# A hybrid diffusion step on one core: the context's output projection and first FFN 2 weights beside the latents' attention, its second weights beside the latents' halves

## The chip, the cores and the metric

The kernel runs on one core of one Trainium2 chip. The metric is device time in microseconds of one execution. One execution was also recorded by the hardware profiler; all rows below come from it. TensorE is called PE in the rows (its weight loads PEld), VectorE DVE, ScalarE ACT, GpSimd POOL; SyncE (SP) issues all the transfers.

## What is computed

One layer of a hybrid backbone over 1024 latent tokens and 256 context tokens, model width 1024, all in fp32. A cut of the reference:

```
h = x + 0.5 * g1 * swiglu(modulate(rms_norm(x, ng[0]), sh1, sc1), ffn_w_in[0], ffn_w_out[0])
mix = mixer(modulate(rms_norm(h, ng[1]), sh2, sc2))     # four groups A, B, C, D of width 256, then @ w_out
h = h + g2 * mix
h = h + 0.5 * g3 * swiglu(modulate(rms_norm(h, ng[2]), sh3, sc3), ffn_w_in[1], ffn_w_out[1])
y = rms_norm(h, final_g)

def swiglu(x, w_in, w_out):
    a, b = jnp.split(x @ w_in, 2, axis=-1)
    return (jax.nn.silu(a) * b) @ w_out
```

Group A is windowed attention, B a long convolution (Hyena), C dense attention, D a gated linear recurrence (GLA). Context tokens see only context. Latents see latents, cached context keys (not those computed here) and given GLA states. So the context's and the latents' rows never need each other after the projections. The FFN's inner width is 2816, 22 blocks of 128.

## The kernel before

Activations lie with the model width on the partitions (8 blocks of 128) and tokens along the columns, in the three chunks of `CHUNKS`: latents 0 to 511, latents 512 to 1023, context (256 columns). A product in fp32 is made of three matmuls of rounded operands: a weight is split into a high part `wh` (ScalarE, line 56) and a low part `wl` (VectorE or GpSimd, line 62), the activation likewise, and `mm3` (lines 986 to 988) adds wh x xh, wh x xl and wl x xh in PSUM.

The kernel is written with a tile framework: pools hand out buffers, and a scheduler places each instruction on its engine's queue. It goes by priority: program order, and `tc.high_priority(offset=LEAD)` with LEAD = 4000 puts a block ahead by that many positions. Two blocks with the same offset keep their program order. Each engine then works its queue strictly in order. A pool with `side="right"` takes memory from the other end; memory and the eight PSUM banks are handed on only when their last reader is done.

The part of the program that the change touches, in program order:

1. Latents' attention and GLA (some 1500 to 1980 us). `run_gla` is written first, at plain priority; `run_attention(..., "lat")` after it at LEAD. Attention is four jobs, A and C with two pairs of heads each; in each, `attn_heads` loads keys and queries and makes each row's maximum (lines 690, 694), and `attn_core` makes scores, exponentials, sums (line 754) and values (line 742); the maxima of the next job run beside the core of the one before. GLA (`gla_prepare`, `gla`) first does the latents, then the context. PSUM: x=2, a=2, s=1, o=1 for attention, g=2 for GLA.
2. The context's output projection, `w_out(2, ...)`, on GLA's two banks, at plain priority. It reads the mixers' outputs (`ysc`), so it needs the context's GLA.
3. Then a new set of banks (l=6, h=1, a=1): the latents' output projection `w_out(0)`, `w_out(1)` with the sums of squares of its result (`sum_rsq`); beside it the context's norm (`norm_mod`).
4. `hidden_ctx`, the first weights of FFN 2 for the context: 22 steps of 48 matmuls of 256 columns, then SiLU (line 1021) and the product (line 1022). Four of its steps stand between the four steps of `halves`, which reads the latents' rows back, norms them (lines 1107, 1108) and splits the seven half-size operands (lines 1116, 62) that `hidden_lat` multiplies by a scheme of seven half-size products in place of eight.
5. `hidden_lat`, the first weights for the latents: 22 steps (some 2232 to 2640 us).
6. `second` for chunk 0, chunk 1 and the context: the second weights, 22 steps of 24 matmuls each, summed in eight banks (four for the context); the inner values come back from memory (`hid`). The final norm `finish(c)` of chunks 0 and 1 stands at steps 2 and 8 of the context's `second`, that of the context at the end. With `on_pe` (the last one) the squares are summed by matmuls (line 913), otherwise by VectorE and GpSimd with one matmul at the end (line 923); the bank comes from "h", which here is an alias of the eight "o" banks. Line 1679 and line 1677 make the output.

Of the kernel before, what the change touches and what calls it, by code (L numbers as in the profile page):

```python
# [9 lines left out]
F32 = mybir.dt.float32  # L10
# [827 lines left out]
def model(tc, i, o):  # L838
# [161 lines left out]
    def half_tiles(p):  # L1000
        return {n: tuple(p.tile([128, 4, 512], F32R, tag=n + r, name=n) for r in "hl") for n in HALVES}

    def hidden_ctx(P, idx, X, keep):

        W = {}

        def prepare(f):
            if f < NFF:
                with tc.high_priority(offset=LEAD if f else 0):
                    W[f] = [load_w(P, i["w1"][idx, f, s], lo_engines=("dve", "dve" if s else "pool"))  # L1010
                            for s in range(2)]
        prepare(0)
        yield
        for f in range(NFF):
            prepare(f + 1)
            ps = E.psum("l").rearrange("p (s t) -> p s t", s=2)
            for s, w in enumerate(W.pop(f)):
                mm3(ps[:, s], w, (at(X[0]), at(X[1])), 8)
            with tc.high_priority(offset=LEAD):
                g = P["t2"].tile([128, 512], F32, tag="t2", name="g")[:, :T_CTX]  # L1020
                nc.scalar.activation(out=g, in_=ps[:, 0], func=ACTF.Silu)
                nc.vector.tensor_tensor(out=g, in0=g, in1=ps[:, 1], op=ALU.mult)
                E.load(keep[f][:, T_LAT:], g)
            yield
# [116 lines left out]
            nc.tensor.matmul(ps, lhsT=E.ones128, rhs=t, start=k == 0, stop=k == 7)  # L1141
        rsqrt_into(E, None, R, ps, 1.0 / 1024, n, tiles=[work() for _ in range(3)], pin=True, sq_engine=nc.vector)

    def second(P, idx, c, keep, h):

        t0, n = CHUNKS[c]
        cd = cond_of(c)
        W = {}

        def prepare(f):  # L1150
            if f < NFF:
                with tc.high_priority(offset=LEAD):
                    g = P["gr"].tile([128, 512], F32, tag="gr", name="g")[:, :n]
                    E.load(g, keep[f][:, t0:t0 + n])
                    if n == 512:
                        gh, gl = (P["gs"].tile([128, 512], F32R, tag="gs", name="gs") for _ in range(2))
                    else:
                        both = P["gs"].tile([128, 512], F32R, tag="gs", name="gs")
                        gh, gl = both[:, :n], both[:, n:2 * n]
                    split_hi_lo(E, g, gh, gl, lo_engine="dve")  # L1160
                    W[f] = load_w(P, i["w2"][idx, f].rearrange("p (k m) -> p k m", k=8),
                                  lo_engines=("dve", "dve")), gh, gl
        per = 512 // n
        prepare(0)
        banks = [E.psum("o") for _ in range(8 // per)]
        for f in range(NFF):
            prepare(f + 1)
            (wh, wl), gh, gl = W.pop(f)
            for d in range(8):
                ps = banks[d // per][:, d % per * n:d % per * n + n]  # L1170
                first = f == 0 and d % per == 0
                mm3(ps, (lambda k: wh(d), lambda k: wl(d)), (lambda k: gh, lambda k: gl), 1, start=first,
                    stop=f == NFF - 1, loose=True)
            if f < NFF - 1:
                yield
        with tc.high_priority(offset=LEAD):
            for d in range(8):
                nc.vector.scalar_tensor_tensor(out=h[:, d], in0=banks[d // per][:, d % per * n:d % per * n + n],
                                               scalar=gates[:, idx, d, cd:cd + 1], in1=h[:, d], op0=ALU.mult, op1=ALU.add)
        yield  # L1180
# [394 lines left out]


    po = ExitStack()
    E.set_banks(po, x=2, a=2, s=1, o=1, g=2)
    ats = ExitStack()
    gls = ExitStack()  # L1580
    run_gla(E, gls)
    gls.close()
    cp = pool(ats, "atc", 1)
    E.ident_r, E.mask_r = cp.tile([128, 128], F32R, name="ident_r"), cp.tile([128, 640], F32R, name="mask_r")
# [7 lines left out]

    fs = ExitStack()
    P = dict(raw=pool(fs, "raw", 4, **R_), wb=pool(fs, "wb", 12, **R_), t2=pool(fs, "t2", 9, **R_))
    cs_ = ExitStack()
    xp2 = pool(cs_, "xn2", 1, **R_)
    Rl = [xp2.tile([128, 512], F32, name=f"rl{c}") for c in range(2)]
    hsc2 = scratch("hsc2", [1024, T_ALL])
    hv2 = hsc2.rearrange("(k p) t -> p k t", p=128)

# [21 lines left out]
            E.load(hv2[:, d, t0:t0 + n], t)  # L1622
            yield t

    h2st = ExitStack()
    h2 = pool(h2st, "h2", 1, **R_).tile([128, 8, T_CTX], F32, name="h2")
    Y = load_y(2, xp2)
    for _ in w_out(2, Y, "g", lambda d: h2[:, d]):
        pass
    ats.close()  # L1630
    po.close()
    po = ExitStack()
    E.set_banks(po, l=6, h=1, a=1)
    h = [None, None, h2]
    with ExitStack() as st:
        xp, hq = pool(st, "xy", 1), pool(st, "hq", 8)
        Y = [load_y(c, xp) for c in range(2)]
        Xc = norm_mod(P, xp2, h, 2, 2)
        for c in range(2):
            exp_ln_tables()  # L1640
            sum_rsq(P, w_out(c, Y[c], "l", lambda d: hq.tile([128, 512], F32, tag="hq", name="hq")), 512, Rl[c],
                    lambda: hq.tile([128, 512], F32, tag="hq", name="rs"))
    h2st.close()
    hst = ExitStack()
    XL = half_tiles(pool(hst, "xs", 1))
    xb = pool(cs_, "xb", 7, **R_)
    run = hidden_ctx(P, 1, Xc, hid[1])
    next(run)
    next(run)
    for _ in halves(P, 2, xb, lambda k, c: hv2[:, k, 512 * c:512 * c + 512], Rl, XL):  # L1650
        next(run)
    for _ in run:
        pass
    cs_.close()
    for _ in hidden_lat(P, 1, XL, hid[1]):
        pass
    po.close()
# [7 lines left out]
    def finish(c):  # L1665
        t0, n = CHUNKS[c]
        exp_ln_tables()
        last = c == len(CHUNKS) - 1
        with tc.high_priority(offset=LEAD if last else 0):
            R = chunk_rsq(P, h, c, xp.tile([128, 8 * n], F32, tag=f"tmp{c}", name="tmp"), on_pe=last)  # L1670
            out = xp.tile([128, 8, n], F32, tag=f"out{c}", name="out")
            for k in (1, 4, 7):
                nc.scalar.activation(out=out[:, k], in_=h[c][:, k], func=ACTF.Copy, scale=fing[:, k:k + 1])
            yv = o["y"].rearrange("(k p) t -> p k t", p=128)
            for k in range(8):
                if k % 3 == 1:
                    nc.gpsimd.tensor_tensor(out=out[:, k], in0=out[:, k], in1=R, op=ALU.mult)
                else:
                    nc.vector.scalar_tensor_tensor(out=out[:, k], in0=h[c][:, k], scalar=fing[:, k:k + 1], in1=R,
                                                   op0=ALU.mult, op1=ALU.mult)  # L1680
                if k % 2:
                    E.load(yv[:, k - 1:k + 1, t0:t0 + n], out[:, k - 1:k + 1])

    for c, (t0, n) in enumerate(CHUNKS):
        h[c] = hp.tile([128, 8, n], F32, name=f"h{c}")
        E.load(h[c], hv2[:, :, t0:t0 + n])
        for f, _ in enumerate(second(P, 1, c, hid[1], h[c])):
            if c == 2 and f in (2, 8):
                finish(f // 6)
    finish(2)  # L1690
    gst.close()
    fs.close()
    po.close()
# [104 lines left out]
```

## Time and profile before

| | us |
|---|---|
| median of 3 runs | 2982.4 (2979.0 to 2985.7) |
| the profiled execution, its own time | 2978.95 |
| its span in the trace | 2977.2 |
| TensorE busy | 2769.8 |
| VectorE busy | 1897.1 |
| ScalarE busy | 1124.9 |
| GpSimd busy | 1108.3 |

Busy means that an instruction of the engine was under way. The granted clock of TensorE is given as a share of 2.4 GHz; 0.50 is 1.2 GHz, and a value between is a mean over both.

### The profile page before, as it was taken

How to read it: one execution, taken by the hardware profiler on the slowest of the kernel's cores; microseconds unless marked ns; L12 is line 12 of the kernel's file. 1: busy time of each engine (PE TensorE's matmuls, PEld its weight loads, DVE VectorE, ACT ScalarE, POOL GpSimd, SP SyncE). 2: the span in 40 equal slices, each digit the busy share in tenths (PEclk: the TensorE clock that was granted, in tenths of full speed). 3: DMA queues.
4: the chain of work that ended last, by engine and by line, in shares of the span. 5: the costliest groups of instructions: out<-in, count | busy, mean ns of one | idle time of the engine just before them, and what ended most of it. 6: DMA issues, size and time to landing. Idle time of an engine off the chain costs nothing. (4 is left out here: it accounts for less than half of the span.)

```text
span 2977.2 us, 39869 instructions
## 1 busy us (share of the span) xinstructions
PE 2769.8 (93%) x14088; PEld 2194.8 (74%) x14088; DVE 1897.1 (64%) x3153; ACT 1124.9 (38%) x2033; POOL 1108.3 (37%) x980
## 2 busy tenths in 40 slices
PE   7899988999999898887988989989999999999998
PEld 5886766788888787785754544567998888878888
DVE  4878677744899945776747566662955545533447
ACT  5742222233233642223424423553743332333444
POOL 1344355543000224555415425463435555520002
PEclk9999999999999999998978969889999999999999
DMA  8654645342877463433362110354652222244445
GB/s 292 213 177 138 211 109 125 93 138 96 292 256 258 167 212 113 145 115 101 104 160 54 41 27 11 110 200 156 216 177 92 85 78 85 85 173 149 147 138 197
DMA packets 278460, 427.02 MB, mean 143 GB/s; under 512 B 97417, under 2 KB 163954, under 8 KB 276852
## 3 DMA queue, kind: packets, MB, share of 16 engines
q1 hardware_dynamic: 278260, 424.47, 44.0%
q8 instruction: 111, 1.82, 0.3%
q14 instruction: 89, 0.73, 0.1%
HBM read 345.14 MB, written 79.13 MB: 143 GB/s over the span
## 5 line engine op out<-in xcount | busy, mean ns | idle before, releaser
L56 ACT ACTIVATE wh<-raw 128x512 fp32r<-128x512 f32 x661 | 409.7, 626 | 531.6 <-PE ps L987 234.1
L62 POOL TENSOR_TENSOR wl<-raw,wh 128x512 fp32r<-128x512 f32 x221 | 321.7, 1459 | 579.6 <-ACT wh L56 356.9
L62 DVE TENSOR_TENSOR wl<-raw,wh 128x512 fp32r<-128x512 f32 x440 | 332.7, 762 | 176.7 <-ACT wh L56 113.2
L987 PE MATMUL ps<-gs,wh 128*128 128x512 f32 (+1 forms) x1056 | 376.8, 358 | 7.1 <-DVE gs L62 7.1
L988 PE MATMUL ps<-gs,wl 128*128 128x512 f32 (+1 forms) x1056 | 374.6, 356 | 2.9 <-DVE wl L62 2.9
L986 PE MATMUL ps<-gs,wh 128*128 128x512 f32 (+1 forms) x1056 | 352.4, 358 | 9.3 <-ACT gs L56 5.0
L986 PE MATMUL ps<-xh,wh 128*128 128x256 f32 (+2 forms) x952 | 324.0, 341 | 14.6 <-ACT sw L1493 10.9
L988 PE MATMUL ps<-xh,wl 128*128 128x256 f32 (+2 forms) x952 | 320.3, 338 | 6.0 <-POOL wl L62 3.1
L987 PE MATMUL ps<-xl,wh 128*128 128x256 f32 (+2 forms) x952 | 325.4, 342 | 0.0
L986 PE MATMUL ps<-t,wh 128*128 128x512 f32 x704 | 281.5, 400 | 17.1 <-DVE up L1079 12.6
L988 PE MATMUL ps<-t,wl 128*128 128x512 f32 x704 | 281.6, 401 | 2.4 <-DVE wl L62 2.4
L987 PE MATMUL ps<-t,wh 128*128 128x512 f32 x704 | 282.5, 401 | 0.0
L986 PEld LDWEIGHTS ps<-gs,wh 128*128 128x128 f32 x1056 | 201.0, 191 | 40.4 <-ACT gs L56 5.4
L56 ACT ACTIVATE wh<-s 128x512 fp32r<-128x512 f32 x176 | 110.6, 631 | 311.0 <-PE ps L987 146.9
L987 PEld LDWEIGHTS ps<-gs,wh 128*128 128x128 f32 x1056 | 201.6, 191 | 36.0 <-DVE gs L62 7.8
L988 PEld LDWEIGHTS ps<-gs,wl 128*128 128x128 f32 x1056 | 200.9, 191 | 32.6 <-DVE wl L62 3.7
L986 PE MATMUL ps<-b,wh 128*128 128x512 f32 x528 | 211.2, 400 | 10.9 <-DVE up L1076 10.9
L986 PEld LDWEIGHTS ps<-xh,wh 128*128 128x128 f32 (+1 forms) x952 | 183.6, 193 | 43.4 <-ACT sw L1493 12.7
L987 PE MATMUL ps<-b,wh 128*128 128x512 f32 x528 | 210.5, 399 | 0.0
L988 PE MATMUL ps<-b,wl 128*128 128x512 f32 x528 | 209.6, 397 | 0.0
L988 PEld LDWEIGHTS ps<-xh,wl 128*128 128x128 f32 (+1 forms) x952 | 183.0, 193 | 31.6 <-issue 5.9
L921 POOL TENSOR_TENSOR tmp<-tmp 128x512 f32<-128x512 f32 (+1 forms) x18 | 24.7, 1371 | 479.7 <-ACT tmp L919 479.7
(367 smaller groups left out, 5915.7 us busy)
## 6 DMA issues: line engine op xcount, KB each, us to landing
raw<-in_w SPq DMA_DIRECT2D x308, 512.0 KB, 3.7
stg<-in_wmT SPq DMA_DIRECT2D x56, 512.0 KB, 4.0
hid<-g SPq DMA_DIRECT2D x88, 256.0 KB, 2.0
g<-hid SPq DMA_DIRECT2D x88, 256.0 KB, 2.7
m<-in_dft_lat SPq DMA_DIRECT2D x128, 128.0 KB, 2.3
raw<-in_wo SPq DMA_DIRECT2D x24, 512.0 KB, 4.1
x<-in_xT SPq DMA_DIRECT2D x36, 256.0 KB, 4.6
stg<-in_wmp SPq DMA_DIRECT2D x16, 512.0 KB, 11.0
```

The lines of the kernel that those rows point to most:

```text
L56: nc.scalar.activation(out=hi, in_=src, func=ACTF.Copy)
L62: low = eng.tensor_tensor(out=lo, in0=src, in1=hi.bitcast(F32), op=ALU.subtract)
L921: eng.tensor_tensor(out=acc, in0=acc, in1=s, op=ALU.add)
L986: nc.tensor.matmul(ps, lhsT=wh(k), rhs=xh(k), start=start and k == 0, stop=False, skip_group_check=loose)
L987: nc.tensor.matmul(ps, lhsT=wh(k), rhs=xl(k), start=False, stop=False, skip_group_check=loose)
L988: nc.tensor.matmul(ps, lhsT=wl(k), rhs=xh(k), start=False, stop=stop and k == nk - 1, skip_group_check=loose)
```

## The change

GLA gets attention's offset. The context's output projection keeps its place, and the context's norm and all of `hidden_ctx` follow it directly, on GLA's banks, before attention's banks are given back; SiLU is made there of exponential and logarithm, the functions that attention uses. The latents' output projection then runs on banks l=3, h=1, and the context's `second` on o=4 beside `halves`: each step of `halves` at LEAD, then five steps of `second`, whose own preparation has no lead. At the end `second` runs for chunks 0 and 1 only; `finish` of the context stands at step 4 of chunk 0, that of chunk 0 at step 4 of chunk 1, that of chunk 1 at the end.

```diff
@@ -1000,7 +1000,7 @@
     def half_tiles(p):
         return {n: tuple(p.tile([128, 4, 512], F32R, tag=n + r, name=n) for r in "hl") for n in HALVES}
 
-    def hidden_ctx(P, idx, X, keep):
+    def hidden_ctx(P, idx, X, keep, bank="l", tables=None):
 
         W = {}
 
@@ -1013,12 +1013,18 @@
         yield
         for f in range(NFF):
             prepare(f + 1)
-            ps = E.psum("l").rearrange("p (s t) -> p s t", s=2)
+            ps = E.psum(bank).rearrange("p (s t) -> p s t", s=2)
             for s, w in enumerate(W.pop(f)):
                 mm3(ps[:, s], w, (at(X[0]), at(X[1])), 8)
             with tc.high_priority(offset=LEAD):
                 g = P["t2"].tile([128, 512], F32, tag="t2", name="g")[:, :T_CTX]
-                nc.scalar.activation(out=g, in_=ps[:, 0], func=ACTF.Silu)
+                if tables == "exp":
+                    nc.scalar.activation(out=g, in_=ps[:, 0], func=ACTF.Exp, scale=-1.0)
+                    nc.scalar.activation(out=g, in_=g, func=ACTF.Ln, bias=1.0)
+                    nc.scalar.activation(out=g, in_=g, func=ACTF.Exp, scale=-1.0)
+                    nc.vector.tensor_tensor(out=g, in0=g, in1=ps[:, 0], op=ALU.mult)
+                else:
+                    nc.scalar.activation(out=g, in_=ps[:, 0], func=ACTF.Silu)
                 nc.vector.tensor_tensor(out=g, in0=g, in1=ps[:, 1], op=ALU.mult)
                 E.load(keep[f][:, T_LAT:], g)
             yield
@@ -1141,7 +1147,7 @@
             nc.tensor.matmul(ps, lhsT=E.ones128, rhs=t, start=k == 0, stop=k == 7)
         rsqrt_into(E, None, R, ps, 1.0 / 1024, n, tiles=[work() for _ in range(3)], pin=True, sq_engine=nc.vector)
 
-    def second(P, idx, c, keep, h):
+    def second(P, idx, c, keep, h, lead=None):
 
         t0, n = CHUNKS[c]
         cd = cond_of(c)
@@ -1149,8 +1155,8 @@
 
         def prepare(f):
             if f < NFF:
-                with tc.high_priority(offset=LEAD):
-                    g = P["gr"].tile([128, 512], F32, tag="gr", name="g")[:, :n]
+                with tc.high_priority(offset=LEAD if lead is None else lead):
+                    g = P["gr"].tile([128, 512 if lead is None else n], F32, tag="gr", name="g")[:, :n]
                     E.load(g, keep[f][:, t0:t0 + n])
                     if n == 512:
                         gh, gl = (P["gs"].tile([128, 512], F32R, tag="gs", name="gs") for _ in range(2))
@@ -1575,10 +1581,11 @@
 
 
     po = ExitStack()
-    E.set_banks(po, x=2, a=2, s=1, o=1, g=2)
+    E.set_banks(po, x=2, a=2, s=1, o=1, g=2, alias=(("h", "g"),))
     ats = ExitStack()
     gls = ExitStack()
-    run_gla(E, gls)
+    with tc.high_priority(offset=LEAD):
+        run_gla(E, gls)
     gls.close()
     cp = pool(ats, "atc", 1)
     E.ident_r, E.mask_r = cp.tile([128, 128], F32R, name="ident_r"), cp.tile([128, 640], F32R, name="mask_r")
@@ -1592,9 +1599,11 @@
 
     fs = ExitStack()
     P = dict(raw=pool(fs, "raw", 4, **R_), wb=pool(fs, "wb", 12, **R_), t2=pool(fs, "t2", 9, **R_))
+    fp = pool(fs, "fp", 1, **R_)
+    Rl = [fp.tile([128, 512], F32, name=f"rl{c}") for c in range(2)]
+    h2 = fp.tile([128, 8, T_CTX], F32, name="h2")
     cs_ = ExitStack()
     xp2 = pool(cs_, "xn2", 1, **R_)
-    Rl = [xp2.tile([128, 512], F32, name=f"rl{c}") for c in range(2)]
     hsc2 = scratch("hsc2", [1024, T_ALL])
     hv2 = hsc2.rearrange("(k p) t -> p k t", p=128)
 
@@ -1622,36 +1631,43 @@
             E.load(hv2[:, d, t0:t0 + n], t)
             yield t
 
-    h2st = ExitStack()
-    h2 = pool(h2st, "h2", 1, **R_).tile([128, 8, T_CTX], F32, name="h2")
     Y = load_y(2, xp2)
     for _ in w_out(2, Y, "g", lambda d: h2[:, d]):
         pass
+    h = [None, None, h2]
+    Xc = norm_mod(P, xp2, h, 2, 2)
+    for _ in hidden_ctx(P, 1, Xc, hid[1], "g", "exp"):
+        pass
+    cs_.close()
     ats.close()
     po.close()
     po = ExitStack()
-    E.set_banks(po, l=6, h=1, a=1)
-    h = [None, None, h2]
+    E.set_banks(po, l=3, h=1, o=4)
+    cs_ = ExitStack()
+    P.update(gs=pool(cs_, "gs", 2, **R_), gr=pool(cs_, "gr", 2, **R_))
+    run = second(P, 1, 2, hid[1], h2, 0)
     with ExitStack() as st:
         xp, hq = pool(st, "xy", 1), pool(st, "hq", 8)
         Y = [load_y(c, xp) for c in range(2)]
-        Xc = norm_mod(P, xp2, h, 2, 2)
         for c in range(2):
-            exp_ln_tables()
             sum_rsq(P, w_out(c, Y[c], "l", lambda d: hq.tile([128, 512], F32, tag="hq", name="hq")), 512, Rl[c],
                     lambda: hq.tile([128, 512], F32, tag="hq", name="rs"))
-    h2st.close()
     hst = ExitStack()
     XL = half_tiles(pool(hst, "xs", 1))
     xb = pool(cs_, "xb", 7, **R_)
-    run = hidden_ctx(P, 1, Xc, hid[1])
-    next(run)
-    next(run)
-    for _ in halves(P, 2, xb, lambda k, c: hv2[:, k, 512 * c:512 * c + 512], Rl, XL):
-        next(run)
+    steps = halves(P, 2, xb, lambda k, c: hv2[:, k, 512 * c:512 * c + 512], Rl, XL)
+    while True:
+        with tc.high_priority(offset=LEAD):
+            if next(steps, 0) == 0:
+                break
+        for _ in range(5):
+            next(run)
     for _ in run:
         pass
     cs_.close()
+    po.close()
+    po = ExitStack()
+    E.set_banks(po, l=6, h=1, a=1)
     for _ in hidden_lat(P, 1, XL, hid[1]):
         pass
     po.close()
@@ -1665,7 +1681,7 @@
     def finish(c):
         t0, n = CHUNKS[c]
         exp_ln_tables()
-        last = c == len(CHUNKS) - 1
+        last = c == 1
         with tc.high_priority(offset=LEAD if last else 0):
             R = chunk_rsq(P, h, c, xp.tile([128, 8 * n], F32, tag=f"tmp{c}", name="tmp"), on_pe=last)
             out = xp.tile([128, 8, n], F32, tag=f"out{c}", name="out")
@@ -1681,13 +1697,13 @@
                 if k % 2:
                     E.load(yv[:, k - 1:k + 1, t0:t0 + n], out[:, k - 1:k + 1])
 
-    for c, (t0, n) in enumerate(CHUNKS):
+    for c, (t0, n) in enumerate(CHUNKS[:2]):
         h[c] = hp.tile([128, 8, n], F32, name=f"h{c}")
         E.load(h[c], hv2[:, :, t0:t0 + n])
         for f, _ in enumerate(second(P, 1, c, hid[1], h[c])):
-            if c == 2 and f in (2, 8):
-                finish(f // 6)
-    finish(2)
+            if f == 4:
+                finish(0 if c else 2)
+    finish(1)
     gst.close()
     fs.close()
     po.close()
```

## Rows read from the trace of the kernel before

**Rows 1.** The page, busy time: engine, busy us (share of span), instructions.
```profile
PE 2769.8 (93%) x14088; PEld 2194.8 (74%) x14088; DVE 1897.1 (64%) x3153; ACT 1124.9 (38%) x2033; POOL 1108.3 (37%) x980
```
**Rows 2.** Windows: width, busy PE, PEld, DVE, ACT, POOL (instructions), PE clock, DMA share, GB/s.
```profile
1500.00:1980.00 480.00, 435.36 (x1969) 240.70 (x1968) 315.97 (x504) 193.19 (x386) 209.47 (x174) 0.85 0.29 82
1500.00:1640.00 140.00, 117.47 (x501) 65.81 (x499) 94.30 (x160) 52.42 (x105) 51.48 (x48) 0.80 0.44 108
1700.00:1770.00 70.00, 62.15 (x234) 32.18 (x232) 42.65 (x80) 20.87 (x49) 18.24 (x19) 0.66 0.26 58
1770.00:1840.00 70.00, 70.00 (x337) 35.81 (x335) 41.45 (x71) 24.16 (x43) 34.92 (x28) 1.00 0.02 5
1840.00:1880.00 40.00, 36.06 (x129) 16.73 (x130) 27.56 (x41) 14.88 (x28) 18.42 (x14) 0.74 0.07 28
1950.00:1980.00 30.00, 20.14 (x96) 15.24 (x95) 23.08 (x29) 15.19 (x32) 15.28 (x12) 0.72 0.64 226
2093.00:2149.00 56.00, 50.22 (x383) 49.01 (x382) 54.98 (x79) 43.03 (x80) 26.38 (x12) 0.94 0.67 227
2149.00:2217.00 68.00, 67.64 (x563) 67.34 (x561) 39.96 (x58) 33.68 (x62) 20.75 (x13) 1.00 0.64 209
2217.00:2232.00 15.00, 12.79 (x47) 9.80 (x48) 11.31 (x10) 5.67 (x11) 11.35 (x7) 0.89 0.24 76
2640.00:2885.00 245.00, 244.12 (x1075) 201.49 (x1075) 99.19 (x149) 86.92 (x147) 7.05 (x5) 1.00 0.47 163
2885.00:2946.00 61.00, 59.00 (x429) 55.95 (x428) 54.89 (x82) 37.00 (x69) 18.84 (x11) 0.97 0.69 236
```
**Rows 3.** Windows of 10 us, 1710 and 1750, the same columns.
```profile
1710.00:1720.00 10.00, 6.96 (x16) 2.41 (x14) 8.15 (x15) 4.93 (x13) 1.10 (x2) 0.79 0.95 160
...
1750.00:1760.00 10.00, 10.00 (x25) 5.57 (x26) 6.48 (x15) 1.19 (x2) 2.51 (x2) 0.50 0.00 0
```
**Rows 4.** One line's or tile's instructions: ns min/median/max, first and last start.
```profile
L552 PE MATMUL ps<-qt,S x160: 272/272/473, 1647.4 to 1898.3; 64*128 64x64 f32 x160
...
L50 SPq DMA_DIRECT2D raw<-in_wo x6: 333/433/737, 1911.7 to 1927.0; - x6
...
L1620 DVE SCALAR_TENSOR_TENSOR h<-ps,mod,h x8: 469/472/486, 1924.7 to 1962.7; 128x256 f32<-128x256 f32 x8
```
**Rows 5.** Groups by line and form, 2149 to 2217: count, busy us, mean ns, idle.
```profile
L62 DVE TENSOR_TENSOR wl<-raw,wh 128x512 fp32r<-128x512 f32 x34 | 25.9, 770 | 14.4 <-ACT wh L56 14.4
L62 POOL TENSOR_TENSOR wl<-raw,wh 128x512 fp32r<-128x512 f32 x11 | 15.9, 1448 | 37.5 <-ACT wh L56 37.5
L1022 DVE TENSOR_TENSOR g<-g,ps 128x256 f32<-128x256 f32 x12 | 5.0, 416 | 9.0 <-ACT g L1021 9.0
```
**Rows 6.** Groups by line and form, 2093 to 2169, VectorE and GpSimd.
```profile
L1107 DVE TENSOR_TENSOR x<-x,rl 128x512 f32<-128x512 f32 x15 | 14.3, 959 | 0.9 <-DMA x<-hsc 0.9
L62 DVE TENSOR_TENSOR t<-d,t 128x512 fp32r<-128x512 f32 x12 | 10.0, 833 | 0.1
...
L1116 DVE TENSOR_TENSOR d<-x,d 128x512 f32<-128x512 f32 x8 | 5.4, 677 | 0.0
L62 DVE TENSOR_TENSOR t<-x,t 128x512 fp32r<-128x512 f32 x4 | 5.4, 1342 | 0.0
...
L62 POOL TENSOR_TENSOR b<-x,b 128x512 fp32r<-128x512 f32 x4 | 16.7, 4172 | 14.0 <-ACT b L56 14.0
```
**Rows 7.** Groups by line and form, 2885 to 2964, the context's second weights.
```profile
L62 DVE TENSOR_TENSOR wl<-raw,wh 128x512 fp32r<-128x512 f32 x43 | 29.2, 693 | 10.2 <-ACT wh L56 10.0
```
**Rows 8.** The end: the chain that ended last (start, us), then groups from 2925.
```profile
2963.85 3.47 PE ps L913 x16
...
L1679 DVE SCALAR_TENSOR_TENSOR out<-h,final_g,R 128x512 f32<-128x512 f32 x5 | 6.5, 1365 | 0.0
...
L1679 DVE SCALAR_TENSOR_TENSOR out<-h,final_g,R 128x256 f32<-128x256 f32 x5 | 3.5, 756 | 0.0
...
L75 DVE TENSOR_SCALAR tmp<-ps 128x512 f32<-128x512 f32 x1 | 0.7, 678 | 0.0
```

## The prediction

> **What bounds the kernel now.** I read the engines' busy shares first, then the windows by stage, then narrow windows inside the bad stages, then the groups by line that the change moves. TensorE is busy for 2769.8 of 2977.2 us [rows 1], so only two things can be won: time in which it idles, and time in which it works at the lower of its two clock levels (1.2 instead of 2.4 GHz). For each stage I take loss = width - busy x granted clock [rows 2]. 1500 to 1640 us: 140 - 117.47 x 0.80 = 46.0. 1700 to 1770: 29.0. 1840 to 1880: 13.3. 1950 to 1980: 15.5. 2093 to 2149: 8.8. 2217 to 2232: 3.6. 2885 to 2946: 3.8. Between these, TensorE is full at full clock (1770 to 1840, 2149 to 2217). So latents' attention with GLA (1500 to 1980) loses 104 us, and everything from there to 2232 another 12.
>
> The losses come as events where one of the four attention jobs (two groups by two head pairs) hands over to the next. The narrow windows show one: TensorE is 7.0 of 10 us busy at 1710, the granted clock is then 0.50, and at 1750 TensorE is busy for the whole window and still at 0.50 [rows 3]. A gap of some 6 us thus costs 29. What could fill such gaps is work that needs nothing of the latents' attention. GLA is such work, but its own chain stops on VectorE at the same moments; its last output matmul is at 1898, and the context's projection, which needs GLA and its memory, loads its first weights at 1911 [rows 4]. So the context's weights can fill only if GLA ends early, and this is what its new priority decides.
>
> **The change part by part.** TensorE's work stays the same: FFN 2's first weights for the context are 1056 matmuls of 256 columns, and 563 of these took 67.64 us [rows 2], 0.12 each, 127 us in all. The second weights for the context are 528 of the same, 63 us. Both only move, so the sum is one of losses.
>
> *GLA ahead of attention.* GLA is written before attention, so at the same offset it comes first. Its pools lie on the side that the context's attention has to leave first, so it can't begin at 1500; its output matmuls ran from 1647 to 1898 behind attention [rows 4]. How early it ends now no row shows. Bounds: 1898, where it ends at lowest priority, and about 1650, where the outputs began; I take 1750, as VectorE, on which both depend, is 67% busy from 1500 to 1640 [rows 2] and GLA's chain is serial. Then the context's projection, whose 51 us (from 1911.7 to its last sum at 1962.7 [rows 4]) lie beside attention, ends near 1800, and the first weights fill from there. The two later events, 13.3 + 15.5 = 28.8, fall to them, and 40% of the one at 1700 (11.6), which GLA-first moves later and where the projection's matmuls already lie about. The first 46 us stay: nothing new is ready.
>
> *First weights beside attention.* Each of 22 steps adds three VectorE subtractions (0.770), one on GpSimd (1.448) and two short ones of the gate [rows 5]: 22 x (3 x 0.77 + 2 x 0.41) = 69 us on VectorE, 32 on GpSimd. From 1500 to 1980 VectorE was busy for 316 of 480 us [rows 2]; with 69 it has 385 in a stage that takes 127 us of work more. It is not the bound, but TensorE runs its queue in order, and a weight that comes late now holds attention's matmuls too: I charge 5 us (bounds: 0, and 20 for one event like the cheaper ones above). The gate's two extra activations a step lie on ScalarE, 193 of 480 us busy in this stage [rows 2]. What remains of the first weights when attention ends covers the change-over to the latents' projection. Sum here: -28.8 - 11.6 + 5 = **-35** (bounds -58, all three events, and -15, the last one only).
>
> *Second weights beside the halves.* Before, halves ran against 127 us of well fed TensorE work; now against 63 us, and halves stand first in the queue. VectorE's share of halves: 16 multiplications of 0.96, 16 differences of 0.68 and 24 low parts of about 0.9 [rows 6]: 48 us. The second weights need 44 low parts of 0.693 [rows 7] and 22 of 256 columns, 0.41 by the gate's row [rows 5]: 40 us of VectorE. The latents' projection before it keeps TensorE full, so of the second weights only what fits their two buffers (2 or 3 steps of 2.9 us, say 8.6) is ready when halves start. While halves take their 48 us of VectorE, the rest gets perhaps a fifth of it, 10 us, which feeds 5 steps or 14 us. TensorE idles 48 - 8.6 - 14 = 25 us, against 12.4 lost here before (8.8 + 3.6): **+12**. Bounds: -12 (no loss at all, the next stage's first products filling in) and +25 (halves at 80% of VectorE take 60 us, then 40 more for the second weights, less 63 of work: 37, against 12.4).
>
> One rule of the Trainium skill speaks against this stage. The rows first: low parts of the same shape take 0.833 us in one group and 1.342 in another, and the four on GpSimd take 4.172 each [rows 6]. The page "SBUF — State Buffer", section "Who interferes with whom", says that a VectorE instruction with two SBUF inputs and a GpSimd one that reads SBUF block each other, the later one waiting for the whole of the earlier. By it VectorE would take the 48 us that the rows give; without it, at 0.68 each, 38, and the term would be 38 - 8.6 - 14 - 12.4 = +3. The rows agree with the rule, so I keep 48.
>
> *The end.* The context's own second stage (2885 to 2946) goes: **-3.8**. The norms of the context and the first half now stand at step 4 of chunks that hold all eight PSUM banks, and the norm draws its bank from the same eight. So its one matmul waits until the chunk is read out: for the context that is between the chunks, where 99 of 245 us of VectorE are used [rows 2] and it is hidden; for the first half it is the very end of the kernel. The last norm itself is now over 512 columns, not 256: the 16 matmuls of the sum took 3.47 us, so about 6.9; the root's six steps take 0.68 each at this width, 4.1, where 256 columns cost about 0.41, 2.5; the five products that end it grow from 5 x 0.756 to 5 x 1.365 [rows 5, 8]. That is 3.4 + 1.6 + 3.0 = 8 us. The first half's norm adds the same products to VectorE and GpSimd, mostly while the last sum is made: 2 of up to 8 us. Together **+10** (bounds +6, +16).
>
> Sum: -35 + 12 - 3.8 + 10 = **-17 us**. The profiled execution took 2978.95 us for a span of 2977.2, so 2962; the median of the runs is 2982.4, 3.4 above it, which gives 2965. I forecast 2963, 0.6% faster. About 0.2% (6 us) is what a measurement of this kernel tells from no change.
>
> **Rivals.**
> *Full cover.* All three events go (-58), halves lose no more than before (0), the tail gets 8: -58 - 3.8 + 8 = -54, 2926 us. For it: from 1770 to 1840, where GLA was at hand, TensorE was full [rows 2]. Against: GLA was also at hand at 1710. Chance 0.20.
> *GLA stays late.* Its chain, not its place, sets its end, the context's work starts at 1850 or later, and only the last event goes: -15.5 + 12 - 3.8 + 10 = +3, 2984 us, no change. For it: GLA's own steps wait for one another. Chance 0.14.
> *VectorE decides the halves.* With halves first and little prepared, the stage takes 60 + 40 us of VectorE for 63 of TensorE: +37 instead of +12 (the 12.4 lost before are not credited, since the first latent products wait too and lose as much again). -35 + 37 - 3.8 + 10 = +8, 2989 us, slower. It decides from the point where halves and second weights cost more than 35 + 3.8 - 10 = 29 us in place of 12. For it: VectorE 54.98 of 56 us busy there already [rows 2]. Against: the next stage's products can start under the second weights' remainder. Chance 0.20, of which the rule above carries a part.
> *Forecast.* Partial cover, -17, own range 2945 to 2976: chance 0.46.
>
> Of the 0.14 a little lies on either side of the bound. Faster 0.67, same 0.13, slower 0.20. The range goes from 2922, just below full cover, to 2992, past the third rival.
>
> **What will show it.** GLA's last output matmul before 1800 and first weights of wo near 1750: right; after 1850: the second rival. The windows between 1800 and attention's end at full clock and busy: right. After the latents' projection, a stretch of about 50 us with VectorE full and TensorE half empty: right as to the halves; over 60 us with little of the second weights in it: the third rival. At the end, two sets of output products behind the last matmul, the span running some 23 us past the start of the sum instead of 13.4 (2977.2 - 2963.85 [rows 8]). The forecast would be wrong above all if GLA, put first, keeps VectorE from attention's maxima and makes the first 46 us grow, which I count as nothing.

## The result, and the profile after

The changed kernel takes 3008.35 us (median of 6 runs, 3000.1 to 3018.6), the kernel before in the same job 2980.7 (6 runs, 2975.7 to 2989.8): ratio 1.0091, 95% interval 1.0065 to 1.0117. It is slower by some 27 us, where 17 us less were forecast, and lies beyond the range's upper end (2992).

The page of the changed kernel, busy time (against [rows 1]):

```profile
PE 2761.6 (92%) x14088; PEld 2186.6 (73%) x14088; DVE 1885.7 (63%) x3175; ACT 1139.1 (38%) x2072; POOL 1119.7 (37%) x980
```

TensorE's work is the same 14088 matmuls, so the 27 us are idle time and lower clock of that engine. Windows of the changed kernel, columns as in [rows 2]:

```profile
1500.00:1980.00 480.00, 431.30 (x2020) 242.21 (x2019) 317.02 (x512) 195.18 (x390) 204.75 (x174) 0.88 0.27 75
1500.00:1640.00 140.00, 117.59 (x524) 68.74 (x523) 93.42 (x159) 49.08 (x101) 49.94 (x46) 0.80 0.43 105
1720.00:1760.00 40.00, 35.01 (x170) 17.40 (x170) 34.33 (x57) 19.79 (x47) 17.79 (x18) 0.91 0.45 101
1840.00:1880.00 40.00, 35.42 (x155) 16.72 (x157) 32.54 (x47) 18.81 (x35) 19.19 (x16) 0.87 0.07 28
1960.00:1980.00 20.00, 7.76 (x32) 6.75 (x33) 13.76 (x23) 8.57 (x20) 6.57 (x8) 0.51 0.16 53
1980.00:2100.00 120.00, 120.00 (x1002) 120.00 (x1002) 57.48 (x103) 73.87 (x147) 28.87 (x23) 1.00 0.63 202
2100.00:2120.00 20.00, 11.34 (x54) 9.54 (x54) 10.29 (x18) 12.31 (x22) 5.41 (x5) 0.74 0.92 320
2222.00:2306.00 84.00, 66.48 (x489) 63.32 (x488) 75.83 (x129) 56.48 (x105) 46.52 (x11) 0.93 0.58 192
2982.00:3010.00 28.00, 7.76 (x19) 3.10 (x17) 18.61 (x19) 5.32 (x9) 10.25 (x7) 0.70 0.40 150
```

Read them as width minus busy times clock. The first 46 us of attention stay (45.9). The event of 29 us at 1700 [rows 2] has shrunk to 8 (1720 to 1760). That at 1840 is 9 now, where it was 13. Then come losses that are new or larger: 16 us between 1960 and 1980, 12 between 2100 and 2120, 22 between 2222 and 2306, 23 at the end. (The kernel before lost 15.5 between 1950 and 1980 [rows 2], but while attention still ran; there its last output starts at 1977.2, here at 1964.7.) Between 1980 and 2100 TensorE is full at full clock: the first weights of FFN 2 for the context run there, after attention and not beside it. The two lines that show why, GLA's last products and the context's first weights (`in_wo`, then `in_w`):

```profile
L552 PE MATMUL ps<-qt,S x160: 272/272/472, 1651.5 to 1893.7; 64*128 64x64 f32 x160
...
L50 SPq DMA_DIRECT2D raw<-in_w x32: 327/328/377, 1936.6 to 2050.0; - x32
L50 SPq DMA_DIRECT2D raw<-in_wo x8: 332/404/705, 1909.5 to 1932.4; - x8
```

GLA ends at 1894 (1898 before, [rows 4]) and the context's projection starts at 1909.5 (1911.7), although GLA now stands ahead of attention. From the chain that ended last (start, us, what):

```profile
1965.86 1.24 PE ps L923 x2
...
1970.16 3.65 DVE t L942 x4
...
2103.36 0.94 SPq L50
...
2106.26 5.03 DMA yr<-ysc
...
2242.67 13.42 POOL b L62
...
2299.83 5.77 issue
...
2982.03 0.87 PE ps L923 x2
...
2988.01 6.52 DVE out L1695 x5
```

The chain runs over the context's norm (lines 923, 942) at 1966 to 1974, over the latents' rows `yr` at 2106, over one GpSimd low part of the halves at 2243, and at the end over the products of chunk 0. The 5.77 us at 2299.83, for which the profile names no cause, end at the first product of `hidden_lat`. Just before it VectorE reads the context's sums out of their banks (line 1184, eight reads):

```profile
2302.96 2.43 DVE L1184 SCALAR_TENSOR_TENSOR h<-ps,gates,h 128x256 f32<-128x256 f32 x6
...
2305.60 0.77 PE L986 MATMUL ps<-t,wh 128*128 128x512 f32 x1 [6.59 <-issue]
```

The last read ends at 2305.39, the product starts 0.21 us later. In all eleven traces in which the context's second weights stand ahead of `hidden_lat` it starts 0.20 to 0.21 us behind that read, after 6.3 to 8.0 us of idle time; where they don't, as in the kernel before, TensorE idles 2.3 to 3.2 us there. This is what a change of banks looks like that waits for their last reader, and the new order of work brings it about; no run took this wait away by itself.

To place the 27 us I measured both profiled executions from the first matmul of line 704 behind 1480 us (1504.1 before, 1508.7 after; it is an early one of the latents' attention), because what comes earlier is the same program (single executions; the last section shows how far these scatter):

| stretch | before | after | less the work moved into it | difference |
|---|---|---|---|---|
| to attention's last output (line 808) | 473.1 | 456.0 | | -17.1 |
| to the last sum of the latents' projection | 106.9 | 257.6 | 127 of first weights | +23.7 |
| to the first product of `hidden_lat` | 134.8 | 83.3 | 127 before, 63 after | +12.5 |
| to the end of the span | 758.3 | 704.9 | 63 of second weights before | +9.6 |

Sum +28.7; the spans less their starts differ by 1501.8 - 1473.1 = 28.7.

### The profile page after: what moved, and what is told of

Same layout as the page of the kernel before. It is cut to its first block, busy times and chain, and to the rows that moved or that the text cites. A ratio compares the mean times of both kernels' runs of the same rounds, so it can differ in the third digit from the quotient of the medians.

```text
span 3010.5 us, 39921 instructions
## 1 busy us (share of the span) xinstructions
PE 2761.6 (92%) x14088; PEld 2186.6 (73%) x14088; DVE 1885.7 (63%) x3175; ACT 1139.1 (38%) x2072; POOL 1119.7 (37%) x980
## 4 chain that ended last, share of the span: by engine, by line
PE 70%; DVE 14%; DMA 7%; issue 3%; POOL 3%; ACT 2%; SPq 1%; DVEq 0%; POOLq 0%; ACTq 0%
PE ps L987 19%; PE ps L986 19%; PE ps L988 19%; DMA kslat<-ks 3%; PE ps L742 2%; PE ps L690 2%; PE ps L764 1%; SPq L50 1%; PE ps L765 1%; PE ps L1147 1%; PE ps L552 1%; PE ps L537 1%; DVE junk L1319 1%; DMA raw<-in_w 1%; DVE wl L62 1%
## 5 line engine op out<-in xcount | busy, mean ns | idle before, releaser
L987 PE MATMUL ps<-gs,wh 128*128 128x512 f32 (+1 forms) x1056 | 376.9, 360 | 16.5 <-DVE gs L62 16.5
L986 PE MATMUL ps<-gs,wh 128*128 128x512 f32 (+1 forms) x1056 | 342.0, 357 | 10.4 <-ACT gs L56 6.1
L987 PEld LDWEIGHTS ps<-xl,wh 128*128 128x128 f32 (+1 forms) x952 | 183.7, 193 | 26.0 <-issue 6.8
```

Source lines behind the costliest of these rows:

```text
L986: nc.tensor.matmul(ps, lhsT=wh(k), rhs=xh(k), start=start and k == 0, stop=False, skip_group_check=loose)
L987: nc.tensor.matmul(ps, lhsT=wh(k), rhs=xl(k), start=False, stop=False, skip_group_check=loose)
```

## Experiments

Ratios are to the kernel before, timed in the same job.

### GLA's place

The kernel before, with GLA at attention's offset and nothing else:

```diff
-    run_gla(E, gls)
+    with tc.high_priority(offset=LEAD):
+        run_gla(E, gls)
```

> The kernel before with one edit: GLA gets attention's offset, nothing else moves. Theory: in the changed kernel GLA's last outputs lay where they lay before (1894 instead of 1898 us), so its chain and not its place sets its end, but attention itself ended some 17 us earlier; that gain belongs to GLA's place alone, because its steps no longer come late into attention's queues. Then this kernel is 17 us faster than before (10 to 21; ratio about 0.994), GLA's last output matmul stays at 1880 to 1900 us. Rival: the early end of attention comes from elsewhere in the change (the context's work that fills the hand-overs), then this kernel is within 4 us of before.

Measured: 2960.1 us, ratio 0.9956 (0.9928 to 0.9984), 13 us less (the interval spans 5 to 21). GLA's last output matmul lies at 1883.4. Its windows:

```profile
1500.00:1980.00 480.00, 440.41 (x2011) 245.81 (x2010) 335.05 (x520) 207.82 (x413) 222.71 (x185) 0.89 0.30 87
1720.00:1760.00 40.00, 36.04 (x166) 17.53 (x167) 37.55 (x65) 17.29 (x37) 16.76 (x15) 0.91 0.36 74
```

The first row of [rows 2] has 435.36 busy at 0.85 for the same stretch. The opposite edit, the changed kernel with `run_gla` at plain priority:

```diff
-    with tc.high_priority(offset=LEAD):
-        run_gla(E, gls)
+    run_gla(E, gls)
```

> The changed kernel with GLA back at plain priority. Theory (GLA's place gives attention's gain by itself): 3008 + 17 = 3025 us, ratio to before about 1.015. Rival (its place does nothing here): 3008 us, ratio 1.009.

Measured: 3016.0 us, ratio 1.0129 (1.0098 to 1.0161), less than expected: 8 us more than the changed kernel by the times, 11 by the ratios. The intervals overlap, so this run alone doesn't show a difference. GLA's place is thus a gain of some 13 us by the first run, with which the second agrees, and the rest of the change costs some 40.

Why GLA ends so late in either place: the changed kernel without the latents' attention.

```diff
-    with tc.high_priority(offset=LEAD):
-        run_attention(E, attn_pools(ats, ""), "lat")
...
-            E.load(t, ysc[k // 2][128 * (k % 2):128 * (k % 2) + 128, t0:t0 + n])
+            E.load(t, ysc[k // 2 if c == 2 else (1, 1, 3, 3)[k // 2]][128 * (k % 2):128 * (k % 2) + 128, t0:t0 + n])
```

> The changed kernel with the latents' attention left out (its rows are read from other groups' outputs), to see GLA without competition. With attention GLA runs from 1561 to 1894 us, 333 us, at either priority. Theory (its own chain on few buffers and two banks sets its end): it still takes 200 us or more. Rival (attention's instructions stand ahead of it in the queues): 140 us or less, near its 105 us of TensorE work.

```profile
L552 PE MATMUL ps<-qt,S x160: 417/418/473, 1589.6 to 1733.5; 64*128 64x64 f32 x160
```

GLA's first matmul lies at 1537.8, its last at 1733.5: 196 us without the latents' attention (200 or more were expected; the rival said 140 or less), against 333 with it. The context's projection follows, its first `in_wo` at 1746.2. So the prediction's 1750 was about what GLA reaches when attention is not there at all; beside attention it takes 137 us more. The 196 us are no floor: TensorE was busy for 140 us of the window 1540 to 1740 at a granted clock of 0.51, the lower level almost throughout, and one product took 0.418 us where it took 0.272 in the changed kernel. What in the chain takes the time, the two banks, the single buffers or the way between engines, was not separated.

Then both kernels without GLA, which asks whether the context's work fills attention's gaps when nothing holds it back. In both, a copy of the given state stands for `run_gla`, and `load_y` reads group B's rows for group D's.

```diff
-        run_gla(E, gls)
...
+        E.load(t, i["s0"].rearrange("z p d -> p z d"))
+        E.load(o["new_s"].rearrange("z p d -> p z d"), t)
...
-            E.load(t, ysc[k // 2][128 * (k % 2):128 * (k % 2) + 128, t0:t0 + n])
+            E.load(t, ysc[(0, 1, 2, 1)[k // 2]][128 * (k % 2):128 * (k % 2) + 128, t0:t0 + n])
```

> The changed kernel with GLA left out (its rows are read from another group's outputs, its new state is a copy of the given one). Theory (only GLA's late end keeps the context's work out of attention's gaps): the context's projection starts before 1650 us instead of 1910, projection and first weights run beside attention, the stretch from 1500 to attention's end loses at most 50 instead of 95 us; then it is at least 15 us faster than the kernel before with GLA left out as well (e8), although the changed kernel with GLA is 27 us slower than its counterpart. Rival (attention's gaps can't be filled by this work, or the work comes only after attention at its low priority): 15 to 30 us slower than e8.

> The kernel before with GLA left out in the same way; the yardstick for e7. GLA's matmuls take about 105 us of TensorE, and some of them fill gaps of attention: 2980 - 105 + 20 to 50 of gaps that then stay open = 2895 to 2925 us. Its context's work is the projection alone beside attention.

Measured: 2845.1 us changed (0.9558, 0.9519 to 0.9597), 2863.0 before (0.9613, 0.9581 to 0.9645): the change is worth 18 us here. The stretch from 1600 to 1900, first of the changed kernel, then of its yardstick:

```profile
1600.00:1900.00 300.00, 296.13 (x1766) 213.07 (x1766) 200.46 (x313) 163.30 (x325) 141.77 (x118) 1.00 0.42 125
```

```profile
1600.00:1900.00 300.00, 274.41 (x1030) 141.03 (x1029) 185.24 (x264) 137.25 (x253) 145.90 (x121) 0.90 0.24 70
```

The losses are 4 and 53 us. The changed kernel loads its first `in_wo` at 1544.7 and `in_w` at 1582.6. The work does fill all of attention's later events; in the kernel with GLA it came too late for them. (Without GLA its own work on the engines is gone too; the two were not separated.) The yardstick was expected at 2895 to 2925: GLA costs 115 to 120 us, more than I gave it.

### What lies bare behind attention

The changed kernel without the context's norm ahead of FFN 2:

```diff
-                    nc.scalar.activation(out=g, in_=ps[:, 0], func=ACTF.Exp, scale=-1.0)
+                    nc.scalar.activation(out=g, in_=ps[:, 0], func=ACTF.Exp, scale=-1.0 / 64)
...
-    Xc = norm_mod(P, xp2, h, 2, 2)
+    Xc = Y
```

> The changed kernel with the context's norm ahead of FFN 2 left out (hidden_ctx multiplies the split outputs of the mixers instead; the exponent is scaled by 1/64 so that it stays finite). Theory: in the changed kernel TensorE loses some 20 us between 1950 and 1980, because the norm of the context follows its projection with nothing else for TensorE; without the norm the first weights follow at once, that stretch loses 6 to 10, and the kernel takes 10 to 14 us less: about 2996, ratio to before 1.0055. Rival (the stretch waits for weights or for the end of attention anyway): same as the changed kernel, 1.009.

Measured: 2988.0 us, ratio 1.0029 (1.0005 to 1.0053), some 18 us less than the changed kernel, more than expected. Its windows there and at the next passage:

```profile
1950.00:1980.00 30.00, 30.00 (x250) 29.76 (x249) 18.61 (x29) 18.31 (x35) 7.57 (x6) 1.00 0.70 237
2070.00:2100.00 30.00, 21.15 (x116) 18.44 (x115) 15.49 (x27) 18.46 (x34) 9.78 (x8) 0.83 0.74 257
```

No idle time and full clock where the changed kernel lost 16 in 20 us; the gap behind `hidden_ctx` is still there. In the kernel before, the same norm (lines 923 to 944, 1980 to 1995) left TensorE no idle time, because the latents' projection stood beside it:

```profile
1977.00:2084.00 107.00, 107.00 (x451) 82.34 (x450) 34.40 (x47) 44.36 (x73) 40.66 (x33) 0.99 0.45 153
```

For that gap by itself, the changed kernel with buffers of their own for the latents' rows:

```diff
-    def load_y(c, p):
+    def load_y(c, p, yt=None):
...
-            t = P["t2"].tile([128, 512], F32, tag="t2", name="yr")[:, :n]
+            t = (yt or P["t2"]).tile([128, 512], F32, tag="yr" if yt else "t2", name="yr")[:, :n]
...
-        xp, hq = pool(st, "xy", 1), pool(st, "hq", 8)
-        Y = [load_y(c, xp) for c in range(2)]
+        xp, hq, yt = pool(st, "xy", 1), pool(st, "hq", 8), pool(st, "yt", 4)
+        Y = [load_y(c, xp, yt) for c in range(2)]
```

> The changed kernel, in which the latents' rows of the mixers' outputs are loaded into four buffers of their own instead of the pool t2 that the gate of hidden_ctx uses. Theory: t2's buffers are handed out in program order, so those loads are issued only at 2104 us, right behind the last gate, and TensorE loses 12 us between 2100 and 2120; with own buffers the loads are issued before 2000 us, that loss falls to 0 to 3, and the kernel takes 2997 us (10 to 12 less; ratio to before 1.0055). Rival (the loads are held by the queue's order or by the memory that attention gives back): loads still after 2090 us, 3008 us.

```profile
1960.00:2000.00 40.00, 20.93 (x137) 19.62 (x138) 28.23 (x48) 24.04 (x51) 11.37 (x12) 0.70 0.54 187
2100.00:2120.00 20.00, 20.00 (x131) 18.18 (x131) 6.23 (x11) 10.69 (x23) 11.77 (x10) 1.00 0.66 210
```

The loads now go out from 1947 to 1975 and not from 2104 on, and the gap closes, so the buffers of `t2` made it. Yet the time is 3004.7 us, ratio 1.009 (1.0059 to 1.0122), the changed kernel's own. The splitting of these rows has moved into the stretch of the norm, 1960 to 2000, which loses 25 us in this trace, with VectorE busy for 28.23 of 40. Both edits together:

> Both edits at once: the context's norm ahead of FFN 2 left out, and the latents' rows loaded into buffers of their own. The first alone gave 2988 us (ratio 1.003), the second alone nothing that shows in the time (1.009), although it closed the stretch of 12 us behind hidden_ctx. Theory: the closed stretch is worth its 11 us, and was hidden by the scatter and by a longer wait at the norm; then this kernel takes 2977 us, ratio 0.999. Rival (what is closed there comes back as a wait in the halves): 2988 us, 1.003.

Measured: 2982.6 us, ratio 1.0034 (1.0011 to 1.0058), the same as without the norm alone. The theory of 11 us gets no support: a closed gap of 12 us is worth less than these timings can tell. In the traces the own buffers save 8 us from attention's last output to the last sum of the latents' projection with the norm (257.6 to 250.0) and 9 without it (240.0 to 230.8); in the second pair attention took 4.5 us more and the stretch to `hidden_lat` 2, which is within the scatter.

### The halves

Halves at plain priority instead of first:

```diff
-        with tc.high_priority(offset=LEAD):
-            if next(steps, 0) == 0:
-                break
+        if next(steps, 0) == 0:
+            break
```

> The changed kernel with the halves at plain priority, so that they stand in program order among the second weights. Theory (VectorE sets the length of this stage, 48 us for the halves and 40 for the second weights): the order changes nothing, 3008 us within 4, and the time from the last sum of the latents' projection to the first product of hidden_lat stays at 80 to 88 us. Rival (halves first starve the second weights): 10 us less or better, 2998 us.

Measured: 3007.7 us, ratio 1.010 (1.0076 to 1.0123); from the last sum to the first product of `hidden_lat` 81.2 us (83.3 in the changed kernel). But the edit changed no order. In the two traces all five engines' queues, the transfers included, hold the same instructions in the same order by line, names and shape. So this is the changed kernel timed once more, and whether halves first starve the second weights was not tested.

In the changed kernel the low part that each step of the halves leaves to GpSimd has become very slow, and one of them lies on the chain:

```profile
L62 POOL TENSOR_TENSOR b<-x,b x4: 1289/7354/20640, 2242.7 to 2294.7; 128x512 fp32r<-128x512 f32 x4
```

The four on VectorE, in the changed kernel and then in the kernel with GLA's place alone (`e1`):

```diff
-            put("b21", k, b21, "pool")
+            put("b21", k, b21)
```

> The changed kernel with the four low parts that the halves leave to GpSimd made on VectorE instead. In the changed kernel these four take 1.3 to 20.6 us each (36.6 in all), where 128x512 takes VectorE 0.68. Theory (they are blocked by VectorE and hold the halves' buffers, and the chain runs over them): 2.7 us more for VectorE, but 13 us of waiting go; the stage gets 6 to 12 us shorter, 2999 us, ratio to before 1.006. Rival (VectorE is the bound, GpSimd waits beside it): 3008 to 3011 us.

> The kernel before with GLA at attention's priority (2960 us, ratio 0.9956) and the halves' four low parts on VectorE instead of GpSimd, where they took 1.5 to 5.6 us each. Theory: of the 12 us that TensorE loses around the halves in that kernel 3 to 6 go: 2956 us, ratio 0.994. Rival (the four are hidden there): 2960 us.

Measured: 2985.2 us, ratio 1.0029 (1.0006 to 1.0051), and 2942.6 us, ratio 0.9884 (0.9861 to 0.9907): 18 and 21 us less by the ratios, far more than the theories gave. But summed over windows of 5 us the first trace loses 21.0 us in the stage of the halves, the changed kernel 24.0; its gain lies in attention, whose last output comes 436.5 us after the first matmul of line 704 instead of 456.0. `halves` serves both FFNs, so the edit was made at one of them at a time (`idx == 2` is FFN 2, `idx == 0` FFN 1), and at both in the kernel before:

```diff
-            put("b21", k, b21, "pool")
+            put("b21", k, b21, "dve" if idx == 2 else "pool")
```

> The changed kernel with the four low parts on VectorE in the halves of FFN 2 alone, the stage that the change touches. With both FFNs' halves so changed it took 2985 us (1.003), but its trace shows only 3 us less loss in the stage of FFN 2's halves (21.0 for 24.0) and the rest some 500 us earlier, in attention. Theory: the edit where the change was made is worth those 3 us: 3005 us, ratio 1.008. Rival (GpSimd's low parts at this place are the cause of the 19 us): 2989 us, 1.003.

> The changed kernel with the four low parts on VectorE in the halves of FFN 1 alone, 1000 us before the stages of the change. Theory: the edit makes the scheduler write another order (3292 rows of TensorE's queue differ from the changed kernel, and they are the same rows as with both edits), and attention in that order loses 12 to 16 us less: 2992 us, ratio 1.004. Rival (the 19 us belong to FFN 2's halves): 3008 us, 1.009.

> The kernel before with the four low parts on VectorE in both FFNs' halves, the counterpart of the changed kernel with the same edit (1.0029). Theory: the other order helps here as well, 2965 us, ratio 0.995, so that the change as a whole costs 0.8% in this order too, as in the first (0.9%). Rival (the order helps the changed kernel alone): ratio 1.000, and the change would cost 0.3%.

Measured: in FFN 2 alone 3004.4 us, ratio 1.0087 (1.0071 to 1.0104); in FFN 1 alone 2986.5, 1.0036 (1.001 to 1.0063); in the kernel before, both, 2947.9, 0.9912 (0.9879 to 0.9944). The stage with the edit in FFN 2 alone:

```profile
2212.00:2294.00 82.00, 64.48 (x487) 62.04 (x486) 78.03 (x132) 56.95 (x105) 14.81 (x7) 0.93 0.60 198
```

GpSimd falls from 46.52 to 14.81 us, VectorE stays at 78.03 of 82, and TensorE has the same 64 to 66 us at 0.93. So the slow low parts waited beside VectorE and were no bound, though the chain ran over one of them. The 18 us come from the edit in FFN 1, which makes the scheduler write TensorE's queue otherwise: in the traces 2753 of its 14088 places, from 135 us on, hold another matmul by line, names and shape, and the order is the same as with both edits. With it attention's last output comes 437.7 us after line 704; FFN 1 itself gains nothing that shows (line 704 is reached at 1502.5 with both edits and at 1508.7 without, within the scatter of these traces: 1498.6 to 1512.8). What in the new order helps attention is open. The kernel before gains more from its new order (2965 us were expected). In that order the whole change costs 1.0029 / 0.9912, 1.2%; in the first order 0.9%, with intervals that overlap.

### The end

The kernel before with only the order of its end changed:

```diff
-        last = c == len(CHUNKS) - 1
+        last = c == 1
...
-    for c, (t0, n) in enumerate(CHUNKS):
+    for c in (2, 0, 1):
+        t0, n = CHUNKS[c]
...
-            if c == 2 and f in (2, 8):
-                finish(f // 6)
-    finish(2)
+            if c < 2 and f == 4:
+                finish(0 if c else 2)
+    finish(1)
```

> The kernel before with only the order of its end changed: the context's second weights first, then the latents' chunks; the norm of the context at step 4 of chunk 0, that of chunk 0 at step 4 of chunk 1, that of chunk 1 at the end. Theory: as in the changed kernel, chunk 0's one sum matmul gets a bank only when chunk 1 is read out, so its products and the wider last norm lie behind the last sum; from the start of the last sum's neighbour to the end 28.6 us instead of 13.4, +15, less 2 to 4 of the context's stage: 12 us slower than before, ratio 1.004. Rival (only the last norm's width costs, the first half's norm is hidden): +8 - 4 = +4 us, ratio 1.0015.

Measured: 2994.5 us, ratio 1.0041 (1.0014 to 1.0068), 12 us more, as expected; the rival's 1.0015 lies at the edge of the interval, and the trace decides. Its sum for chunk 0 starts at 2948.1 and the span ends at 2976.7, 28.6 us; the last 28 us of the changed kernel look the same:

```profile
2948.00:2976.00 28.00, 7.98 (x20) 3.27 (x18) 18.84 (x19) 5.32 (x9) 10.24 (x7) 0.70 0.40 150
```

## Why the prediction was wrong, point by point

**GLA ahead of attention: the step that failed.** The prediction took GLA's end as 1750, between 1650 and 1898; it was 1894. The context's work, which needs it, came when attention was nearly over, and with that fell the term of -35: the first two stretches of the table together are -17.1 + 23.7 = +6.6, 42 of the 46 us between the forecast and the trace's difference. The step's second half was right: without GLA the same work saved 53 - 4 = 49 us of loss between 1600 and 1900 and the change gained 18 us. "GLA's chain is serial" stood in the argument, as a reason not to go below 1750; its length was never estimated. [rows 4] gave a hint: 160 products in 251 us, where 0.272 each would take 44. Without attention the chain took 196 us, beside it 333 to 345 in both kernels and at either priority.

**The rival "GLA stays late"** named what happened, with a chance of 0.14, and was priced at +3. It credited the event at 1950 with 15.5 us. But work that comes when attention is over does not fill that event, and the change takes the cover from the context's norm: before, the latents' projection ran beside it; after, TensorE waits for it, 18 us by timing. That exposed chain is the term which no case of the prediction had. The prediction asked what the moved work covers, and not what covers the moved work's own preparation.

**A gain not foreseen.** GLA's place alone saves some 13 us, although GLA then ends only 15 us earlier (1883.4), about as much as attention itself gains. It was counted at nothing. What in attention gains by it is open: the event at 1720 to 1760 loses 7 us where the kernel before loses 22, but that event also changes between executions of one order (last section).

**Second weights beside the halves: +12, measured +12.5** (table). VectorE fits as the mechanism, with 75.83 of 84 us busy, and giving it GpSimd's four low parts made the stage no longer; no run shows it as the bound, since the one on the order changed none. That the sum came out was partly luck: the halves' instructions took 0.68 us each, not the 0.96 and 0.9 that I charged, so nearer 38 than 48 us; the preparation of `hidden_lat`, in the same stretch, was not counted, nor were the 6.6 us for which TensorE idles ahead of `hidden_lat`, at the change of banks (2.3 before). The third rival, +37, did not come.

**The end: +10 - 3.8, measured +9.6** in the table and +12 alone. The mechanism is as written, the size at the upper bound: from the start of the neighbour's sum to the end 28.6 us against 13.4, +15. I gave the first half's products 2 of up to 8 us; on VectorE they stand ahead of the last root, from 2988.01 to 2994.53, while the last sum was ready at 2989.76.

**The sum in timed parts:** GLA's place -13, the end with the context's stage +12, the norm +18, the halves +12.5 by the trace: 29.5, against 27 measured; with intervals of 8 to 10 us to either side of each timed part, that it closes so well is partly chance. The fastest kernel of the study leaves the rest of the change out: GLA's place and the low parts on VectorE, 2942.6 us.

## What to carry to other kernels

Before work is moved behind a dependency, find out how long that dependency's chain takes, by itself and beside what it shares the engines with: here a higher priority moved its end by 15 us at most, where 148 were counted on. Then look for what the moved work uncovers where it used to stand, here a norm that another product hid. And when an edit gains more than its stage loses, try it at each place of its use: the gain may be a new order of the queues elsewhere. When an edit of the order changes nothing, compare the queues first: it may have left them as they were.

## What the runs showed of the hardware

In the halves of the changed kernel two of GpSimd's four low parts of 128x512 took 13.4 and 20.6 us, the other two 1.3. Each long one lies beside a run of VectorE instructions that follow one another without a pause. The runs end at 2254.93 and 2293.62, and GpSimd's instruction ends 1.15 and 1.16 us later. None of the 55 VectorE instructions beside the two took over 0.69 us. The prediction cited the Trainium skill, page "SBUF — State Buffer", section "Who interferes with whom": a VectorE instruction with two SBUF inputs and a GpSimd one that reads SBUF block each other. These rows agree that GpSimd is blocked, and for far longer than one VectorE instruction. VectorE paid at other moments: at the end of the same stage five of its instructions took 0.96 to 1.77 us beside GpSimd's, and in the kernel before 16 between 2093 and 2169 took 0.82 to 1.80. So the 48 us that I kept because of that rule were too many for this stage.

One and the same order scatters by more than the effects sought. The kernel before ran between 2961.7 and 2992.2 us over all jobs. The kernel of the last experiment (the end) has the same TensorE queue up to the latents' second weights; in its profiled execution attention's last output came 460.7 us after the first matmul of line 704, in that of the kernel before 473.1. From 1720 to 1760 the granted clock is 0.66 in the one (both levels) and 0.50 in the other (the lower level throughout), at 35.30 and 35.18 us busy. So a difference of 12 us in attention between two single traces proves nothing, and the -17.1 of the table is one of that kind; the values above for GLA's place are from repeated timings.
